# Reciprocal square roots as a power on POOL in a two-layer hybrid decoder trunk

## The chip, the cores and the metric

The kernel runs on one core of a Trainium2 chip. The metric is the device time of one execution in microseconds (us); of the kernel before the median of three runs is 1027.44. Engines are named as in the profile: PE or TensorE (matmul), PEld (its weight load), DVE or VectorE, ACT or ScalarE, POOL or GpSimd, SP or SyncE (it issues the weights' transfers). `L401` is line 401 of the kernel before; the changed kernel has line numbers of its own.

## The reference

A trunk of two decoder layers over 256 tokens of 1024 features, all in float32. A layer, cut to what matters:

```
xn = rms_norm(h) ;  u = xn @ W_in
o_A = RG-LRU branch ; o_B = Conformer branch (a norm inside)
o_C = differential attention, 4 heads:
      q, k = rope(rms_norm(q)), rope(rms_norm(k))        # per head of 64
      o = rms_norm((softmax1 - lambda * softmax2) @ v)   # per head of 128
o_D = sparse attention, 4 heads: rms_norm of q, k and the indexer's key
h += W_o(sum_j sigmoid(xn @ W_g[j]) * (o_j @ W_b[j]))
h += W_down(silu(g) * v),  [g, v] = dwconv3(rms_norm(h) @ W_up)
h += sigmoid(rms_norm(h) @ W_pg) * rms_norm(p @ W_p)

def rms_norm(x, gain):
    y = x * lax.rsqrt(mean(x * x) + 1e-6)
    return y * gain
```

## The kernel before, in words

**The main stream.** All weights, 340 pieces of mostly 128 x 1024 numbers, pass once through TensorE. SP fetches a piece to `raw` (5 buffers), ACT rounds it to `hi` (`L244`), VectorE subtracts to `lo` (`L245`); `hi` and `lo` have 6 buffers each, and pieces are prepared 3 ahead of their use (`LEAD`). A product is the sum of three: hi by hi, hi by lo, lo by hi (`mm3`, `L317` to `L319`, with the 256 tokens as columns, and `tok_unit`, `L360` to `L362`, with 512 features as columns). Its result lies in one of four PSUM banks (`mm`); four more banks (`sp`) serve all the rest.

**The side work.** The branches are generators: `side_a` (RG-LRU), `side_b` and `conv` (Conformer), `side_c` (differential attention), `side_d` (sparse attention). Between the pieces of the main stream `pump` advances them, each by its own interval (`EVERY`). So their small instructions lie between the main stream's, on the same engines. A scheduler then fixes one queue for each engine, in order; an instruction that waits holds up all that stands behind it in its queue.

**Where the roots are.** `root` (`L400`) makes 1/sqrt(scale * sums + bias) from an ACT root (`L401`) and a VectorE reciprocal (`L402`). It is called ten times on 128 x 2: in `Norm.finish`, in `rnorm` and for the norm of the PLE gate. In `rnorm` and after a norm TensorE first sums the squares over partitions (`L408`), then `root`, then TensorE spreads the two columns over all partitions (`spread`, `L395`). `side_d` has a root over 128 x 12 (`L690`, `L691`), `side_c` one over 128 x 32, for two blocks of 128 tokens, q and k, 8 heads each (`L838`, `L839`), and one over 128 x 8 for the attention's results (`L922`, `L923`). ACT loads a table (ACT_TABLE_LOAD) when the function that it needs next is not in the one that it has.

**`side_c` around the roots.** The squares are made on ACT (`L835`) and summed on VectorE (`L836`), block by block. Behind the root, `L841` makes `qs`, the factors of the queries, from it; ACT applies the factors of the keys head by head (`L850`). The attention's scores (`L881`) need both; `L885` and `L886` take the maximum, `L890` makes the exponentials, `L893` to `L897` the difference of the two softmaxes. `L903` transposes it, and `L911` multiplies by the values. `L916` squares the results, which the root `L922` turns to factors, and `L929` applies these.

**Beside it.** `side_d` makes its indexer's scores on TensorE (`L737`) into four `sp` banks, ACT takes them out (`L741`), VectorE weighs and sums them (`L745`, `L747`) and finds the largest (`L754`, `L755`). `L1010` is a step of the Conformer's convolution on VectorE; `L1092` adds a branch's product on ACT.

Of the kernel before, what the change touches and what calls it, by code (L numbers as in the profile page):

```python
# [10 lines left out]
F32 = mybir.dt.float32  # L11
F32R = mybir.dt.float32r
BF16 = mybir.dt.bfloat16
AF = mybir.ActivationFunctionType
ALU = mybir.AluOpType
# [3 lines left out]
P = 128  # L19
# [110 lines left out]
def decoder_kernel(ctx: ExitStack, tc: tile.TileContext, w_dram, x_dram, xt_dram, p_dram, vec_dram, row_dram,  # L130
                   gain_dram, lru_dram, const_dram, out_dram):
    nc = tc.nc
    A, V, T = nc.scalar, nc.vector, nc.tensor

    cst = ctx.enter_context(tc.tile_pool(name="cst", bufs=1))
# [16 lines left out]
    def bt(tag="big", bufs=NBIG, dtype=F32):  # L152
        return big.tile([P, 2, S], dtype, name=nm("b"), tag=tag, bufs=bufs)

    def st(shape, tag, bufs=1, dtype=F32):
        return sm.tile(shape, dtype, name=nm("s"), tag=tag, bufs=bufs)
# [18 lines left out]
    h = [[cst.tile([P, 512], F32, name=f"h{b}{n}", tag=f"h{b}{n}") for n in range(2)] for b in range(2)]  # L175
# [7 lines left out]
    eps = cst.tile([P, 3], F32, name="eps", tag="eps")  # L183
    V.memset(eps[:, 0:1], EPS)
    V.memset(eps[:, 1:2], 4 * EPS)

    def cc(name):
        o, w = _C[name]
        return con[:, o:o + w]
# [208 lines left out]
        return rs  # L398

    def root(rt, sums, scale, bias):  # L400
        A.activation(rt, sums, AF.Sqrt, scale=scale, bias=bias)  # L401
        V.reciprocal(rt, rt)  # L402

    def rnorm(acc, scale, bias):

        t = smbank()
        for b in range(2):
            T.matmul(t[:, 0, b:b + 1], acc[:, 0, b * P:(b + 1) * P], ones[:, 0:1], start=True, stop=True)  # L408
        rt = st([P, 2], "rt", 4)
        root(rt, t[:, 0, 0:2], scale, bias)  # L410
        return rt, spread(rt)

    class Norm:
# [40 lines left out]
        def finish(self):  # L454
            self.rt = st([P, 2], "rt", 4)
            V.tensor_tensor(self.ss[:, 0, :], self.ss[:, 0, :], self.ss[:, 1, :], op=ALU.add)
            root(self.rt, self.ss[:, 0, :], 1.0 / D, eps[:, 0:1])
# [115 lines left out]
    for l in range(L):  # L573
# [79 lines left out]
        def weave(gens):  # L653

            live = list(gens)
            while live:
                for g in list(live):
                    if next(g, "end") == "end":
                        live.remove(g)
                    else:  # L660
                        yield
# [15 lines left out]
        def side_d():  # L677
            dq, dk, ik = raws["dq"], raws["dk"], raws["ik"]
            ms = st([P, 2, 6], "msd", 1)
            for b in range(2):  # L680
# [6 lines left out]
                j = st([P, P], "junk", 2)  # L687
                A.activation(j[:, 0:32], ik[b][:, 0:32], AF.Square, scale=32 ** -0.5, accum_out=ms[:, b, 5:6])
                yield
            A.activation(ms, ms, AF.Sqrt, bias=eps[:, 0:1])  # L690
            V.reciprocal(ms, ms)  # L691
            qs = st([P, 2, 4], "qsd", 1)
            V.tensor_scalar(qs, ms[:, :, 0:4], P ** -0.5, None, op0=ALU.mult)
            yield
# [134 lines left out]
        def side_c():  # L829
            cq, ck, cv = raws["cq"], raws["ck"], raws["cv"]  # L830
            ms = st([P, 2, 2, 8], "msc", 1)
            for b in range(2):
                for i, t in enumerate((cq, ck)):
# [1 line left out]
                    A.activation(j, t[b], AF.Square, scale=0.125)  # L835
                    V.tensor_reduce(ms[:, b, i, :], j.rearrange("p (h w) -> p h w", h=8), axis=AX.X, op=ALU.add)  # L836
                    yield
            A.activation(ms, ms, AF.Sqrt, bias=eps[:, 0:1])  # L838
            V.reciprocal(ms, ms)  # L839
            qs = st([P, 2, 8], "qs", 1)  # L840
            V.tensor_scalar(qs, ms[:, :, 0, :], 0.125, None, op0=ALU.mult)  # L841
            yield
# [23 lines left out]
            mo = st([P, 2, 4], "mo", 1)  # L866
# [52 lines left out]

            yield from weave([*two_heads(1), attend(0, (0, 1))])  # L920
            yield from weave(attend(1, (hp,)) for hp in range(2))
            A.activation(mo, mo, AF.Sqrt, bias=eps[:, 0:1])  # L922
            V.reciprocal(mo, mo)  # L923
            oc = [(bt(dtype=F32R), bt(dtype=F32R)) for _ in range(2)]
            o_pairs[2] = oc
            for b in range(2):
# [4 lines left out]
            for b in range(2):  # L931
# [4 lines left out]
                for i in range(2):  # L936
# [3 lines left out]
                                           op1=ALU.subtract)  # L940
# [120 lines left out]
        t = st([80, S], "ikc", 1)  # L1061
# [96 lines left out]
        for g2 in range(NG // 2):  # L1158
            cf = st([P, 4, S], "e4", 2)
            pair = bt()  # L1160
            for q in range(2):
# [7 lines left out]
                for s_ in range(2):  # L1169
                    c = g + s_ * NG  # L1170
                    A.activation(cf[:, 2 * q + s_, :], bank[:, s_, :], AF.Identity, scale=w[:, 3 * c + 2:3 * c + 3],  # L1171
                                 bias=bb[:, c:c + 1])
                for d in (1, 2):
                    for s_ in range(2):
                        c = g + s_ * NG
                        t = cf[:, 2 * q + s_, d:]
                        V.scalar_tensor_tensor(t, bank[:, s_, :S - d], w[:, 3 * c + 2 - d:3 * c + 3 - d], t,  # L1177
                                               op0=ALU.mult, op1=ALU.add)
# [28 lines left out]
        for n in range(2):  # L1207
# [5 lines left out]
            for b, c, bank in parts:  # L1213
                cs = slice(c, c + bank.shape[1])
                t = bt().rearrange("p a b -> p (a b)")[:, cs]
# [104 lines left out]
```

## Time and profile before

| | |
|---|---|
| median of 3 runs | 1027.44 us (1027.05 to 1027.67) |
| the profiled execution | 1026.79 us, its span 1025.0 us |
| granted TensorE clock | 1.00 |
| PE busy | 1017.8 us |
| DVE busy | 832.1 us |
| ACT busy | 687.3 us |
| POOL busy | 0.2 us |
| HBM | 182.46 MB read, 179 GB/s over the span |

The span is what the profile sees of the execution, the rest of its time lies ahead of the first instruction and behind the last. Busy times are sums over the whole span; what a stage waits for is read from that stage. The profile's page has five parts that matter here: busy times, the chain that ended last, the costliest groups, the waits, and the timeline of a window, where a row in brackets tells how long the engine stood idle ahead of it and what ended that.

### The profile page before, as it was taken

Reading aid. Unit: us, or ns where it says so; the run is one execution under the profiler, and the core shown is the slowest. Engines: PE = TensorE matmul, PEld = TensorE weight load, DVE = VectorE, ACT = ScalarE, POOL = GpSimd, SP = SyncE. Lnnn points to the kernel's source line nnn. Section 1 sums busy time; section 2 is a strip of 40 time slices with the busy share of each in tenths; the row PEclk is TensorE's granted clock in tenths of the full one; section 3 lists DMA queues with packets and bytes.
Section 4 is the critical chain, followed back from the end, with each engine's and each line's share of the span. In section 5 each row is a group of like instructions: output and inputs, shape, how many; then the busy total and the mean of one; then the engine's idle time right before and its main releaser. Section 6 shows DMA issues by size and latency. Waiting matters only on the chain.

```text
span 1025.0 us, 16548 instructions
## 1 busy us (share of the span) xinstructions
PE 1017.8 (99%) x6108; PEld 896.5 (87%) x6108; DVE 832.1 (81%) x1530; ACT 687.3 (67%) x1190; POOL 0.2 (0%) x4
## 2 busy tenths in 40 slices
PE   9999999999999999999999999999999999999998
PEld 9988787888889999988899887888788899999887
DVE  7898999968869988765676989999687899887454
ACT  8688685977467766554765786859764776665443
POOL 0000000000000000000000000000000000000000
PEclk9999999999999999999999999999999999999999
DMA  8665844653538566476653657445446466566651
GB/s 288 236 192 167 278 140 146 184 161 121 199 108 305 160 206 188 145 256 188 189 178 119 207 167 224 144 147 183 144 153 196 144 207 184 186 186 185 188 162 42
DMA packets 53936, 184.58 MB, mean 180 GB/s; under 512 B 6112, under 2 KB 8160, under 8 KB 53856
## 3 DMA queue, kind: packets, MB, share of 16 engines
q1 hardware_dynamic: 53712, 183.52, 57.1%
q8 instruction: 48, 0.79, 0.3%
q14 instruction: 32, 0.26, 0.1%
q10 hardware_dynamic: 144, 0.00, 0.0%
HBM read 182.46 MB, written 1.05 MB: 179 GB/s over the span
## 4 chain that ended last, share of the span: by engine, by line
PE 92%; DVE 4%; ACT 2%; issue 1%; DMA 1%; SPq 0%; ACTq 0%
PE mm L360 17%; PE mm L361 17%; PE mm L362 17%; PE mm L319 11%; PE mm L317 11%; PE mm L318 11%; DVE lo L245 1%; PE mm L383 1%; DVE b L1010 1%; PE sp L451 1%; PE sp L797 1%; PE sp L911 1%; PE sp L881 1%; DVE s L755 1%; PE sp L821 1%
## 5 line engine op out<-in xcount | busy, mean ns | idle before, releaser
L244 ACT ACTIVATE hi<-raw 128x1024 fp32r<-128x1024 f32 (+1 forms) x340 | 352.8, 1048 | 210.4 <-PE mm L362 128.0
L245 DVE TENSOR_TENSOR lo<-raw,hi 128x1024 fp32r<-128x1024 f32 (+1 forms) x340 | 407.4, 1206 | 98.9 <-ACT hi L244 96.8
L360 PE MATMUL mm<-hi,b 128*128 128x512 f32 x848 | 337.2, 398 | 0.1
L361 PE MATMUL mm<-lo,b 128*128 128x512 f32 x848 | 330.8, 390 | 0.0
L362 PE MATMUL mm<-hi,b 128*128 128x512 f32 x848 | 330.3, 390 | 0.0
L319 PE MATMUL mm<-b,lo 128*128 128x256 f32 x960 | 271.4, 283 | 0.5 <-DVE lo L245 0.4
L317 PE MATMUL mm<-b,hi 128*128 128x256 f32 x960 | 271.4, 284 | 0.3 <-DVE b L440 0.2
L318 PE MATMUL mm<-b,hi 128*128 128x256 f32 x960 | 271.0, 283 | 0.0
L360 PEld LDWEIGHTS mm<-hi,b 128*128 128x128 f32 x848 | 159.4, 188 | 35.3 <-issue 1.1
L362 PEld LDWEIGHTS mm<-hi,b 128*128 128x128 f32 x848 | 159.2, 188 | 33.7
L361 PEld LDWEIGHTS mm<-lo,b 128*128 128x128 f32 x848 | 159.5, 188 | 31.5 <-issue 0.5
L319 PEld LDWEIGHTS mm<-b,lo 128*128 128x128 f32 x960 | 184.1, 192 | 1.2 <-DVE lo L245 1.1
L317 PEld LDWEIGHTS mm<-b,hi 128*128 128x128 f32 x960 | 183.7, 192 | 1.2 <-DVE b L440 0.6
L318 PEld LDWEIGHTS mm<-b,hi 128*128 128x128 f32 x960 | 184.1, 192 | 0.3 <-DVE b L441 0.2
L1010 DVE SCALAR_TENSOR_TENSOR b<-s,vec,b 128x256 f32<-128x256 f32 x240 | 104.8, 475 | 0.0
L1177 DVE SCALAR_TENSOR_TENSOR s<-mm,vec,s 128x255 f32<-128x255 f32 (+1 forms) x144 | 59.7, 474 | 5.7 <-ACT s L1171 5.7
L303 ACT ACTIVATE b<-b 128x512 fp32r<-128x512 f32 x40 | 25.0, 626 | 21.4 <-DVE b L1181 19.0
L1171 ACT ACTIVATE s<-mm,vec 128x256 f32<-128x256 f32 x72 | 36.1, 551 | 2.5 <-PE mm L319 2.5
L304 DVE TENSOR_TENSOR b<-b,b 128x512 fp32r<-128x512 f32 x40 | 27.4, 687 | 12.6 <-ACT b L303 12.6
L890 ACT ACTIVATE s<-sp,s,s 128x128 f32<-128x128 f32 (+1 forms) x32 | 15.9, 512 | 15.2 <-DVE s L886 14.9
L491 DVE TENSOR_TENSOR b<-mm,s 128x512 f32<-128x512 f32 x24 | 16.3, 683 | 11.1 <-PE mm L319 11.0
L1180 ACT ACTIVATE s<-s 128x256 f32<-128x256 f32 x44 | 17.8, 409 | 10.0 <-DVE s L1177 10.0
(229 smaller groups left out, 783.2 us busy)
## 6 DMA issues: line engine op xcount, KB each, us to landing
raw<-in_w_dram SPq DMA_DIRECT2D x332, 512.0 KB, 4.2
raw<-in_w_dram SPq DMA_DIRECT2D x8, 256.0 KB, 5.0
b<-in_x_dram SPq DMA_DIRECT2D x8, 128.0 KB, 4.5
b<-in_lru_dram SPq DMA_DIRECT2D x4, 256.0 KB, 4.9
h<-in_xt_dram SPq DMA_DIRECT2D x4, 256.0 KB, 6.2
gain<-in_gain_dram SPq DMA_DIRECT2D x2, 512.0 KB, 5.8
out_dram<-h SPq DMA_DIRECT2D x3, 256.0 KB, 2.3
row<-in_row_dram SPq DMA_DIRECT2D x2, 272.0 KB, 5.5
```

The costliest lines, as they stand in the source:

```text
L244: A.activation(hi[:, cs], raw[:, cs], AF.Copy)
L245: last_lo[0] = V.tensor_tensor(lo[:, cs], raw[:, cs], hi[:, cs].bitcast(F32), op=ALU.subtract).ins
L304: V.tensor_tensor(lo, src, hi.bitcast(F32), op=ALU.subtract)
L317: T.matmul(out, a, xh, start=first and k == 0, stop=False)
L318: T.matmul(out, a, xl, start=False, stop=False)
L319: T.matmul(out, b, xh, start=False, stop=last and k == nk - 1)
L360: T.matmul(outs[b], xk[k][0][:, bs], wh[:, kk, :], start=k == 0, stop=False)
L361: T.matmul(outs[b], xk[k][0][:, bs], wl[:, kk, :], start=False, stop=False)
L362: T.matmul(outs[b], xk[k][1][:, bs], wh[:, kk, :], start=False, stop=last)
L1010: V.scalar_tensor_tensor(t, ypad[:, c, d:d + S], w[:, 31 * c + d:31 * c + d + 1], t, op0=ALU.mult, op1=ALU.add)
L1171: A.activation(cf[:, 2 * q + s_, :], bank[:, s_, :], AF.Identity, scale=w[:, 3 * c + 2:3 * c + 3], bias=bb[:, c:c + 1])
L1177: V.scalar_tensor_tensor(t, bank[:, s_, :S - d], w[:, 3 * c + 2 - d:3 * c + 3 - d], t, op0=ALU.mult, op1=ALU.add)
```

## The change

A tile `half_power` of 16 columns of -0.5 is made once. `root` is now a VectorE `tensor_scalar` (times scale, plus bias) and, on POOL, a `tensor_tensor` with `pow` of it and `half_power`, in place. The three roots of the attentions go through a new function `roots`, which calls `root` for each block of 128 tokens, so 128 x 12 becomes two of 128 x 6, 128 x 32 two of 128 x 16, 128 x 8 two of 128 x 4. That makes 22 powers in all: 10 of 2 columns, 4 each of 6, 16 and 4. The square root of the RG-LRU (`L986`) stays on ACT. On ACT 16 table loads are left of 36.

```diff
--- before.py
+++ after.py
@@ -184,6 +184,9 @@
     V.memset(eps[:, 0:1], EPS)
     V.memset(eps[:, 1:2], 4 * EPS)
 
+    half_power = cst.tile([P, 16], F32, name="half_power", tag="half_power")
+    V.memset(half_power, -0.5)
+
     def cc(name):
         o, w = _C[name]
         return con[:, o:o + w]
@@ -398,8 +401,13 @@
         return rs
 
     def root(rt, sums, scale, bias):
-        A.activation(rt, sums, AF.Sqrt, scale=scale, bias=bias)
-        V.reciprocal(rt, rt)
+        V.tensor_scalar(rt, sums, scale, bias, op0=ALU.mult, op1=ALU.add)
+        nc.gpsimd.tensor_tensor(rt, rt, half_power[:, 0:rt.shape[1]], op=ALU.pow)
+
+    def roots(t):
+
+        for b in range(2):
+            root(t[:, b, :], t[:, b, :], 1.0, eps[:, 0:1])
 
     def rnorm(acc, scale, bias):
 
@@ -687,8 +695,7 @@
                 j = st([P, P], "junk", 2)
                 A.activation(j[:, 0:32], ik[b][:, 0:32], AF.Square, scale=32 ** -0.5, accum_out=ms[:, b, 5:6])
                 yield
-            A.activation(ms, ms, AF.Sqrt, bias=eps[:, 0:1])
-            V.reciprocal(ms, ms)
+            roots(ms)
             qs = st([P, 2, 4], "qsd", 1)
             V.tensor_scalar(qs, ms[:, :, 0:4], P ** -0.5, None, op0=ALU.mult)
             yield
@@ -835,8 +842,7 @@
                     A.activation(j, t[b], AF.Square, scale=0.125)
                     V.tensor_reduce(ms[:, b, i, :], j.rearrange("p (h w) -> p h w", h=8), axis=AX.X, op=ALU.add)
                     yield
-            A.activation(ms, ms, AF.Sqrt, bias=eps[:, 0:1])
-            V.reciprocal(ms, ms)
+            roots(ms.rearrange("p b i h -> p b (i h)"))
             qs = st([P, 2, 8], "qs", 1)
             V.tensor_scalar(qs, ms[:, :, 0, :], 0.125, None, op0=ALU.mult)
             yield
@@ -919,8 +925,7 @@
 
             yield from weave([*two_heads(1), attend(0, (0, 1))])
             yield from weave(attend(1, (hp,)) for hp in range(2))
-            A.activation(mo, mo, AF.Sqrt, bias=eps[:, 0:1])
-            V.reciprocal(mo, mo)
+            roots(mo)
             oc = [(bt(dtype=F32R), bt(dtype=F32R)) for _ in range(2)]
             o_pairs[2] = oc
             for b in range(2):
```

Since the factors of a block no longer wait for those of the other, and since ACT has fewer instructions, the scheduler writes the queues in another order. Three places follow. Names left of the arrow are written, those right of it read.

**ACT's queue at the root of `side_c`, layer 0, before** (`s_1451` are the factors, `L741` takes the scores of `side_d` out of PSUM):

```order
L244 ACTIVATE hi_1573<-raw_1572 128x1024
L741 ACTIVATE s_1487<-sp_1475 128x256
L741 ACTIVATE s_1487<-sp_1476 128x256
L741 ACTIVATE s_1487<-sp_1477 128x256
L741 ACTIVATE s_1487<-sp_1478 128x256
L1092 ACTIVATE b_1548<-mm_1399,s_507 128x512
L1092 ACTIVATE b_1550<-mm_1400,s_507 128x512
L835 ACTIVATE b_1598<-b_1293 128x512
L244 ACTIVATE hi_1602<-raw_1601 128x1024
L838 ACT_TABLE_LOAD
L838 ACTIVATE s_1451<-s_1451,eps 128x32
L741 ACTIVATE s_1535<-sp_1523 128x512
```

and now (`L748` is what `L741` was, `L856` what `L850` was, `L842` what `L835` was, `L1097` what `L1092` was; `s_1455` are the factors):

```order
L247 ACTIVATE hi_1577<-raw_1576 128x1024
L856 ACTIVATE b_1295<-b_1295,s_1455 128x64
L748 ACTIVATE s_1491<-sp_1479 128x256
L748 ACTIVATE s_1491<-sp_1480 128x256
L748 ACTIVATE s_1491<-sp_1481 128x256
L748 ACTIVATE s_1491<-sp_1482 128x256
L856 ACTIVATE b_1295<-b_1295,s_1455 128x64 x7
L1097 ACTIVATE b_1552<-mm_1403,s_509 128x512
L1097 ACTIVATE b_1554<-mm_1404,s_509 128x512
L842 ACTIVATE b_1602<-b_1297 128x512
L247 ACTIVATE hi_1606<-raw_1605 128x1024
L748 ACTIVATE s_1539<-sp_1527 128x512
```

Eight `L856`, which read the factors of the first block of tokens, now stand among the work of `side_d`, one of them ahead of the first four `L748`, and seven ahead of `L1097` and `L842`. The table load is gone.

**VectorE's queue at the same place, before** (`L841` reads the factors, `L839` is the reciprocal):

```order
L245 TENSOR_TENSOR lo_1603<-raw_1601,hi_1602 128x1024
L750 TENSOR_TENSOR s_1473<-s_1473,con 128x128
L550 TENSOR_TENSOR s_4935<-s_4935 128x4
L754 MAX s_1650<-s_1473 128x8
L839 RECIPROCAL s_1451<-s_1451 128x32
L755 MATCH_REPLACE s_1474<-s_1650,s_1473 128x128
L841 TENSOR_SCALAR s_1625<-s_1451 128x16
L745 TENSOR_SCALAR s_1521<-s_1535,s_1207 128x256
```

and now (`L404` is the new `tensor_scalar`, of the second block; `L847` is what `L841` was, `L754` what `L747` was):

```order
L248 TENSOR_TENSOR lo_1607<-raw_1605,hi_1606 128x1024
L752 TENSOR_SCALAR s_1525<-s_1539,s_1211 128x256
L404 TENSOR_SCALAR s_1455<-s_1455,eps 128x16
L754 SCALAR_TENSOR_TENSOR s_1525<-s_1539,s_1211,s_1525 128x256
L847 TENSOR_SCALAR s_1631<-s_1455 128x16
L757 TENSOR_TENSOR s_1477<-s_1477,con 128x128
L754 SCALAR_TENSOR_TENSOR s_1525<-s_1540,s_1211,s_1525 128x256
```

Between the root's own instruction and the reader of the factors stood one `MATCH_REPLACE`, now one `L754`; the power itself is in POOL's queue, between the two.

**ACT's queue at the second block of queries of the differential attention, layer 0, before** (`L890` are the exponentials):

```order
L916 ACTIVATE s_2187,s_1855<-b_1853 128x128
L1092 ACTIVATE b_2235<-mm_2083,s_507 128x512
L1092 ACTIVATE b_2237<-mm_2084,s_507 128x512
L778 ACTIVATE b_1204<-sp_2207,vec_75 128x2x128
L778 ACTIVATE b_1205<-sp_2207,vec_75 128x2x128
L781 ACTIVATE s_1206<-sp_2214 128x128
L244 ACTIVATE hi_2327<-raw_2326 128x1024
L890 ACTIVATE s_2218,s_2217<-sp_2219,s_2217,s_1625 128x256 x2
L890 ACTIVATE s_2218,s_2217<-sp_2220,s_2217,s_1625 128x256 x2
```

and now (`L922` is what `L916` was, `L934` what `L929` was, `L896` what `L890` was, `L785` and `L788` what `L778` and `L781` were; `s_1861` are the factors of the results):

```order
L922 ACTIVATE s_2193,s_1861<-b_1859 128x128
L1097 ACTIVATE b_2241<-mm_2089,s_509 128x512
L934 ACTIVATE b_1859<-b_1859,s_1861 128x128
L1097 ACTIVATE b_2243<-mm_2090,s_509 128x512
L785 ACTIVATE b_1208<-sp_2213,vec_75 128x2x128
L785 ACTIVATE b_1209<-sp_2213,vec_75 128x2x128
L788 ACTIVATE s_1210<-sp_2220 128x128
L247 ACTIVATE hi_2333<-raw_2332 128x1024
L934 ACTIVATE b_1859<-b_1859,s_1861 128x128 x3
L896 ACTIVATE s_2224,s_2223<-sp_2225,s_2223,s_1631 128x256 x2
L896 ACTIVATE s_2224,s_2223<-sp_2226,s_2223,s_1631 128x256 x2
```

The four `L934` of the first block of tokens, which read its power, moved from behind the attention into this place, the first of them between the two `L1097`. On VectorE the `tensor_scalar` ahead of that power stands behind the `lo` of a piece and ahead of the maxima `L891` (before `L885`) of this block.

On TensorE, `spread` at the start of layer 1 (`L395`) stands 13 matmuls earlier than before, and in `rnorm` of both layers the sum `L408` stands four matmuls earlier, with 3 matmuls of the main stream between it and `L395`, where 7 were. POOL's queue had four memsets; now it has the 22 powers behind them, and ahead of the first power one instruction (ISA) that names the library of the code it needs.

## Rows read from the trace of the kernel before

**Rows 1.** The page, part 1: busy time, share of the span and instructions of each engine.

```profile
PE 1017.8 (99%) x6108; PEld 896.5 (87%) x6108; DVE 832.1 (81%) x1530; ACT 687.3 (67%) x1190; POOL 0.2 (0%) x4
```

**Rows 2.** The waits of TensorE: us in total, times, the longest.

```profile
PE mm L319 <- DVE lo L245: 0.4, 2, 0.2
PE sp L903 <- DVE s L897: 0.4, 1, 0.4
PE sp L395 <- DVE s L402: 0.3, 1, 0.3
```

**Rows 3.** Lines 401, 402, 839: duration ns min/median/max, first and last start.

```profile
L401 ACT ACT_TABLE_LOAD  x6: 1283/1283/1283, 17.6 to 1000.0; - x6
...
L402 DVE RECIPROCAL s<-s x10: 155/166/166, 19.5 to 1001.7; 128x2 f32<-128x2 f32 x10
...
L839 DVE RECIPROCAL s<-s x2: 334/338/343, 132.0 to 646.2; 128x32 f32<-128x32 f32 x2
```

**Rows 4.** Groups of instructions on POOL: busy us, mean ns of one.

```profile
L1308 POOL MEMSET const-float32-0.0<- 128x1 f32 x1 | 0.1, 98 | 0.2 <-issue 0.2
```

**Rows 5.** Busy time by window, layer 0 from `side_c` to the first `L903`.

```profile
123.00:178.00 55.00, 55.00 (x285) 44.38 (x283) 54.54 (x176) 38.52 (x79) 0.00 (x0) 1.00 0.47 149
```

**Rows 6.** Timeline of layer 0 around `side_c`: start us, duration us, [idle before <-releaser].

```profile
124.50 1.19 ACT L741 ACTIVATE s<-sp 128x256 f32<-128x256 f32 x4
126.45 1.37 ACT L1092 ACTIVATE b<-mm,s 128x512 f32<-128x512 f32 x2 [0.77 <-PE mm L362]
127.72 0.62 ACT L835 ACTIVATE b<-b 128x512 f32<-128x512 f32 x1
...
132.74 0.83 ACT L850 ACTIVATE b<-b,s 128x64 f32<-128x64 f32 x3
...
122.08 1.21 DVE L245 TENSOR_TENSOR lo<-raw,hi 128x1024 fp32r<-128x1024 f32 x1
...
125.77 0.28 DVE L745 TENSOR_SCALAR s<-s,s 128x128 f32<-128x128 f32 x1
...
129.44 0.68 DVE L836 TENSOR_REDUCE s<-b 128x8 f32<-128x512 f32 x1
...
133.03 0.47 DVE L747 SCALAR_TENSOR_TENSOR s<-s,s,s 128x256 f32<-128x256 f32 x1
...
127.03 1.15 PE L737 MATMUL sp<-s,s 32*128 32x256 f32 x16
```

**Rows 7.** The same around the second block of queries of the differential attention.

```profile
188.88 1.24 ACT L1092 ACTIVATE b<-mm,s 128x512 f32<-128x512 f32 x2
...
190.89 1.07 ACT L244 ACTIVATE hi<-raw 128x1024 fp32r<-128x1024 f32 x1
192.70 0.57 ACT L890 ACTIVATE s<-sp,s,s 128x256 f32<-128x256 f32 x1 [0.73 <-DVE s L886]
...
193.26 0.55 ACT L890 ACTIVATE s<-sp,s,s 128x256 f32<-128x256 f32 x1
...
230.88 0.68 ACT L929 ACTIVATE b<-b,s 128x128 f32<-128x128 f32 x2
...
189.84 1.21 DVE L245 TENSOR_TENSOR lo<-raw,hi 128x1024 fp32r<-128x1024 f32 x1
...
195.26 1.14 PE L881 MATMUL sp<-b,b 64*128 64x256 f32 x8
```

**Rows 8.** The same in layer 1, VectorE.

```profile
635.30 1.23 DVE L245 TENSOR_TENSOR lo<-raw,hi 128x1024 fp32r<-128x1024 f32 x1 [0.95 <-ACT hi L244]
...
686.40 1.22 DVE L245 TENSOR_TENSOR lo<-raw,hi 128x1024 fp32r<-128x1024 f32 x1 [0.60 <-ACT hi L244]
```

**Rows 9.** The same at the first norm, TensorE.

```profile
18.36 0.50 PE L408 MATMUL sp<-ones,b 128*128 128x1 f32 x4
...
21.53 0.60 PE L395 MATMUL sp<-con,s 128*128 128x128 f32 x4
```

**Rows 10.** The page, part 6: DMA issues, KB each, median us to landing.

```profile
raw<-in_w_dram SPq DMA_DIRECT2D x332, 512.0 KB, 4.2
```

## Prediction, made before the changed kernel was run

> **What bounds the kernel now.** I read the busy times first. TensorE is busy for 1017.8 of the span's 1025.0 us and VectorE for 832.1; POOL, the engine that gets the new work, for 0.2 [rows 1]. So at most 7.2 us can be won anywhere, and then only where TensorE stands still. The view of its waits came next: 0.4 us behind `lo` of `L245`, 0.4 behind `L897`, and 0.3 behind the reciprocal of a norm, at the start of layer 1 [rows 2]. Only that last one is a wait for a root. Of the operations that go, the reader should see that none is expensive for TensorE: the table loads take 1.283 us each, all on ACT, and the reciprocals 0.16 to 0.34 us on VectorE [rows 3].
>
> Then I asked which engine has no slack behind TensorE. From 123 to 178 us VectorE is busy for 54.54 of 55.00 us [rows 5], and at the end of this stretch TensorE waits for it at `L903` [rows 2]. A microsecond that VectorE loses in there is a microsecond that TensorE loses. Layer 1 repeats the stretch with two idle times of VectorE in it, 0.95 and 0.60 us, both behind `hi` of `L244` [rows 8].
>
> **The unknown price.** No row shows a power on any engine. POOL's nearest row is a memset of one column, 98 ns [rows 4]. For a short elementwise operation whose time hardly grows with its columns the nearest rows are VectorE's reciprocals: 0.166 us for 2 columns, 0.338 for 32, under 6 ns a column [rows 3]. The low end is therefore 0.1 us whatever the width. As the high end I take two memsets for a column and two for the start, 0.2 + 0.2n. Below 0.1 us nothing is to be had, since the shortest row of POOL takes that. A power is no single multiply or add, so I expect a cost for each column, and take **one memset for the start and one for each column, 0.1 + 0.1n us**: 0.3 for the norms' 2 columns, 0.5 for the differential attention's 4, 0.7 for the sparse attention's 6, 1.7 for `side_c`'s 16.
>
> What a two-input elementwise instruction costs on this engine is in the Trainium skill (GPSIMD Engine Reference, 3.1 Elementwise): about 2.6 cycles an element, and VectorE roughly twice as quick. No run here shows it. Applied to the power it gives an estimate of 35 ns for 16 columns over the start, so the sum would be that of the cheap rival below; the same section tells writers to leave elementwise work to VectorE.
>
> **Layer 0, `side_c` (16 columns).** Terms (a) to (d) are delays of VectorE between 123 and 178 us.
>
> (a) The first power can start when VectorE is done with `L245` (122.08 + 1.21 = 123.29) and with the new `tensor_scalar` (0.16, as the reciprocal): 123.45. It ends at 125.15. ACT's queue now has an `L850` that needs it ahead of the four `L741`, which began at 124.50 [rows 6]. With its 0.28 (0.83 for three) they begin at 125.43: 0.9 late. The first ends about 125.85; `L745`, which needs it, began at 125.77. Cost 0.1. The last ends at 125.43 + 1.19 = 126.6, before TensorE wants its bank for `L737` at 127.03 [rows 6], so TensorE itself is spared.
>
> (b) Then seven more `L850` (7 x 0.28 = 1.9) stand ahead of the two `L1092` (1.37) and `L835` (0.62): 126.6 + 1.9 + 1.4 + 0.6 = 130.5. VectorE came to `L836`, which needs `L835`, at 129.44 [rows 6]; with (a), (d) and the multiplications of a rotation that now stand ahead it comes at about 129.9. Cost 0.6.
>
> (c) The second power is issued behind `L836`. `L841` needs it, and only one `L747` (0.47) now lies between the `tensor_scalar` and `L841`. VectorE stands still for 1.7 - 0.45 = 1.25, with all its queue behind it.
>
> (d) Four more `tensor_scalar` and two reciprocals less: 4 x 0.16 - 0.2 - 0.33 = 0.1. Some of the next layer's small constants move ahead of `L897`, two of 0.16. Together 0.4, rounded down to 0.3, as issues overlap.
>
> Sum 0.1 + 0.6 + 1.25 + 0.3 = 2.25, which arrives whole at `L903`.
>
> **Layer 0, attention (4 columns).** The squares of the first block of queries used to wait for those of the second. Now VectorE makes their `tensor_scalar` behind `L245` (189.84 + 1.21 = 191.05), so the power ends at 191.05 + 0.16 + 0.5 = 191.7. ACT has an `L929` that needs it right behind the first `L1092` (188.88 + 0.57 = 189.45) and stands for 2.25 us. Behind it wait the second `L1092` and all up to the end of `L244`, 189.45 to 191.96, which is 2.5 us of work, and the four `L929`, 0.68 for two, in a row about 0.3 apart [rows 7]. The first `L890` so begins at 191.7 + 0.3 + 2.5 + 0.9 = 195.4 and not 192.70: 2.7 late. The second `L881` writes at 195.26 + 0.27 into a bank that the second `L890` gives free at 193.26 + 0.55 = 193.81 [rows 7]: 1.7 of slack. Cost 2.7 - 1.7 = 1.0.
>
> **Layer 1.** The same with three differences. `L1092` loses a table load ahead of `L835`, so I leave out (b). (a) is 0.2. VectorE's idle 0.60 us in front of `L245` takes as much of the delay back; the 0.95 lies ahead of the power's harm and takes nothing [rows 8]. So 0.2 + 1.25 + 0.3 - 0.6 + 1.0 = 2.15.
>
> **The norms (2 columns) and `side_d` (6).** `tensor_scalar` and power take 0.16 + 0.3; the pair before took a root on ACT and a reciprocal of 0.17, and in six of ten cases a table load of 1.28 as well [rows 3]. The first norm has from 18.86 to 21.53 for it [rows 9]. At the start of layer 1 `L395` moves 13 matmuls forward while the load ahead of it goes: I leave the wait at its 0.3 [rows 2]. In `rnorm` 3 matmuls instead of 7 lie between `L408` and `L395`: I put 0.2 each on that, an estimate from the 0.3 that the power takes itself. `L474`, which halves a norm's factors on VectorE, now stands for those 0.3 us with the next `lo` behind it, but outside the stretch that is full [rows 5] pieces are ready ahead of their use, and I put nothing on it. In `side_d` an `L992` lies between the power and VectorE's use of it, and I put 0.1 on both layers. Sum 0.5. The table loads that vanish (36 in ACT's queue before, 16 after: 20 x 1.283 = 25.7 us [rows 3]) count as nothing, since ACT is not what TensorE waits for; if they had cover to give, it is spent in (b).
>
> **Sum:** 2.25 + 1.0 + 2.15 + 0.5 = **5.9 us**. The profiled execution took 1026.79 (its span 1025.0 and 1.8 around it), so it would take 1032.7; it lies 0.65 below the median of 1027.44, on which the forecast is **1033.3**. Low end of the price (0.1): (a), (b), (c) are nothing, (d) stays in layer 0 and goes into idle time in layer 1, the attention costs 1.0 - 0.4 = 0.6 in each: 0.3 + 0.6 + 0.6 = 1.5, 1028.9. High end (3.4 for 16 columns, 1.0 for 4): (a) 1.7, (b) 0.6, (c) 2.95, (d) 0.3, attention 1.5, together 7.05; layer 1 1.7 + 2.95 + 0.3 - 0.6 + 1.5 = 5.85; norms 1.1: 14 us, 1041.4.
>
> **Rivals.** *A power as cheap as the low end*: +1.5, 1028.9. For it speaks the slow growth of VectorE's own rows [rows 3].
>
> *Not slower.* If the power of 4 columns is there before ACT comes to `L929`, that is if VectorE's queue runs 2 us earlier against ACT than in rows 7, the attention costs nothing; and if 16 columns take under 0.45, (c) neither. Then the freed ACT can take the 0.3 of `L395` and the 0.4 of `L319` [rows 2] away: -0.7, 1026.7, which is no change that can be measured. Against it: in both layers `L245` and the `tensor_scalar` stand ahead of that power.
>
> *A dear power*, or one that each time waits for a VectorE instruction of the length of `L245`, 1.21 [rows 6], about the high end: 1041.4.
>
> *The first power is late.* Its code may have to be fetched; POOL's queue has a load of it ahead of the first power. A fetch like the weights' takes 4.2 us from issue to landing [rows 10]; the cover at the first norm is 21.53 - 18.86 - 0.16 - 0.3 = 2.2 [rows 9]. If it begins only there, 2.0 come on top: 1035.3. The Trainium skill (GPSIMD Engine Reference, 2.1 Instruction dispatch) gives about 6 us for the first call of freshly loaded code; by that estimate it would be 1037.1. No row shows such a load.
>
> **How the numbers follow.** Forecast 0.52, cheap 0.20, not slower 0.08, dear 0.13, first power late 0.07. A measurement tells about 0.2%, 2.05 us, from no change, so "same" is up to 1029.5: three quarters of the cheap case and most of the not-slower case, 0.21. Faster, 0.04: all the waits of rows 2 together would not reach it, so it needs something that no row shows. Slower 0.75. The range goes from 1028.0, which leaves out "not slower" and a little of the cheap case, to 1042.0, just over the high end.
>
> **What would show it.** POOL's rows give the price: 16 columns near 1.7 us, 4 near 0.5. Right steps: `L841` waits for POOL about 1.2 us in each layer; the first `L903` waits about 2 us longer in layer 0; ACT's `L929` waits for POOL about 2 us; TensorE stands at the second `L881`. ACT's busy time falls by about 25 us and the time does not. Wrong: 16 columns under 0.5 us, or TensorE with no longer stalls at `L903` and `L881`.

## The result, and the profile after

The changed kernel takes 1044.94 us (median of 4 runs, 1044.66 to 1045.25) against 1027.24 before (4 runs): 1.0173 times as long, 95% interval 1.016 to 1.0185. That is 17.7 us slower. The forecast was slower, 1033.3 us, with a range to 1042: the sign was right, the size less than half of what came, and the time lies outside the range.

The page of the changed kernel, the lines that answer to [rows 1]: busy times, the granted clock of TensorE in 40 slices, and the chain that ended last.

```profile
PE 1026.2 (98%) x6108; PEld 903.5 (87%) x6108; DVE 834.4 (80%) x1537; ACT 660.1 (63%) x1154; POOL 30.0 (3%) x26
...
PEclk9999989999999999999999999999999999999999
...
PE 74%; DVE 15%; ACT 5%; issue 2%; POOL 2%; DMA 1%; SPq 0%; DVEq 0%; POOLq 0%; ACTq 0%
```

The span grew from 1025.0 to 1043.2 us, by 18.2. TensorE has the same 6108 instructions, yet is busy for 1026.2 us and not 1017.8: 8.4 us of the 18.2 lie in its busy time, mostly in matmuls that last longer. The other 9.8 are time in which it stands (1043.2 - 1026.2 = 17.0 against 1025.0 - 1017.8 = 7.2). The row PEclk shows why the matmuls are longer: slice 6 (from about 130 us) has an 8 where every slice had a 9; the falls in layer 1 are too short to show there and come out in the windows below. Over the whole span the mean granted clock is 0.993, and it was 1.00: 0.007 x 1043.2 = 7.3 us of full speed are missing. ACT's busy time fell from 687.3 to 660.1 us, and it bought nothing.

The waits of TensorE, to be read beside [rows 2] (us in total, times, the longest; `L744` is what `L737` was, `L909` what `L903` was, `L398` `L395`, `L887` `L881`):

```profile
PE sp L744 <- ACT s L748: 4.2, 2, 2.5
PE sp L909 <- DVE s L903: 4.0, 2, 2.4
PE sp L398 <- POOL s L405: 1.9, 3, 1.0
...
PE sp L887 <- ACT s L896: 0.9, 1, 0.9
```

Four places, 11.0 us. What POOL took for its powers, from the timeline of POOL (start, duration, [idle before]):

```profile
19.41 0.70 POOL L405 TENSOR_TENSOR s<-s,half_power 128x2 f32<-128x2 f32 x1 [18.96 <-DVE s L404]
...
91.01 3.00 POOL L405 TENSOR_TENSOR s<-s,half_power 128x6 f32<-128x6 f32 x2 [70.90 <-DVE s L404]
...
125.11 2.90 POOL L405 TENSOR_TENSOR s<-s,half_power 128x16 f32<-128x16 f32 x1 [31.10 <-DVE s L404]
...
197.76 1.01 POOL L405 TENSOR_TENSOR s<-s,half_power 128x4 f32<-128x4 f32 x1 [59.13 <-DVE s L404]
...
644.66 3.74 POOL L405 TENSOR_TENSOR s<-s,half_power 128x16 f32<-128x16 f32 x1 [30.96 <-DVE s L404]
```

0.70 us for 2 columns, 1.5 for 6, 1.01 for 4, 2.90 to 3.74 for 16. The forecast's sum had 0.3, 0.7, 0.5 and 1.7.

The timeline of the changed kernel at the places of the forecast (VectorE, ACT, then TensorE):

```profile
92.75 0.25 DVE L709 SCALAR_TENSOR_TENSOR s<-s,s,row 128x32 f32<-128x32 f32 x1 [1.08 <-POOL s L405]
...
124.81 0.23 DVE L404 TENSOR_SCALAR s<-s,eps 128x16 f32<-128x16 f32 x1
...
126.30 1.23 DVE L248 TENSOR_TENSOR lo<-raw,hi 128x1024 fp32r<-128x1024 f32 x1
...
128.70 0.29 DVE L752 TENSOR_SCALAR s<-s,s 128x128 f32<-128x128 f32 x1 [1.17 <-ACT s L748]
...
132.85 0.69 DVE L843 TENSOR_REDUCE s<-b 128x8 f32<-128x512 f32 x1 [0.30 <-ACT b L842]
...
138.67 0.17 DVE L847 TENSOR_SCALAR s<-s 128x16 f32<-128x16 f32 x1 [2.79 <-POOL s L405]
...
128.05 0.35 ACT L856 ACTIVATE b<-b,s 128x64 f32<-128x64 f32 x1 [3.60 <-POOL s L405]
...
198.80 0.40 ACT L934 ACTIVATE b<-b,s 128x128 f32<-128x128 f32 x1 [2.61 <-POOL s L405]
...
128.72 2.89 PE L744 MATMUL sp<-s,s 32*128 32x256 f32 x16 [1.77 <-ACT s L748]
...
134.27 0.63 PE L363 MATMUL mm<-hi,b 128*128 128x512 f32 x1
...
185.25 1.12 PE L909 MATMUL sp<-con,s 128*128 128x128 f32 x4 [1.50 <-DVE s L903]
...
204.85 0.48 PE L363 MATMUL mm<-hi,b 128*128 128x512 f32 x1
...
649.11 1.95 PE L744 MATMUL sp<-s,s 32*128 32x256 f32 x16 [2.46 <-ACT s L748]
...
705.15 1.17 PE L909 MATMUL sp<-con,s 128*128 128x128 f32 x4 [2.45 <-DVE s L903]
```

and the same instructions of TensorE before, where [rows 6, 7] do not have them:

```profile
178.61 0.33 PE L903 MATMUL sp<-con,s 128*128 128x128 f32 x1 [0.40 <-DVE s L897]
...
196.48 0.48 PE L360 MATMUL mm<-hi,b 128*128 128x512 f32 x1
...
637.71 1.15 PE L737 MATMUL sp<-s,s 32*128 32x256 f32 x16
...
688.74 0.33 PE L903 MATMUL sp<-con,s 128*128 128x128 f32 x1
```

The starts, set side by side, show how the delay of TensorE grows:

| instruction of TensorE | before | after | later by |
|---|---|---|---|
| second group of `L737` / `L744`, layer 0 | 127.03 | 128.72 | 1.7 |
| `L903` / `L909`, layer 0 | 178.61 | 185.25 | 6.6 |
| first main matmul behind the second block of queries | 196.48 | 204.85 | 8.4 |
| second group of `L737` / `L744`, layer 1 | 637.71 | 649.11 | 11.4 |
| `L903` / `L909`, layer 1 | 688.74 | 705.15 | 16.4 |
| end of the span | 1025.0 | 1043.2 | 18.2 |

A stand of TensorE does not end when the awaited instruction comes. Windows of the changed kernel behind the stands (busy time and instructions of each engine; the number behind the brackets of POOL is the granted clock):

```profile
131.00:137.00 6.00, 6.00 (x18) 4.33 (x16) 4.57 (x12) 4.71 (x9) 1.49 (x1) 0.58 0.16 23
187.00:195.00 8.00, 8.00 (x44) 6.79 (x43) 8.00 (x14) 7.10 (x16) 0.00 (x0) 1.00 0.69 205
651.00:656.00 5.00, 5.00 (x16) 3.98 (x16) 4.75 (x19) 4.97 (x11) 0.17 (x1) 0.66 0.00 0
705.00:711.00 6.00, 5.85 (x19) 4.45 (x20) 6.00 (x12) 5.43 (x9) 0.00 (x0) 0.72 0.70 190
```

Behind the two stands at `L744` and behind the one at `L909` in layer 1 the granted clock is 0.58 to 0.72 over 5 or 6 us, a mixture of its two levels, 1.2 and 2.4 GHz. In the timeline a matmul of 512 columns then lasts 0.63 us (row 134.27) and not 0.39, as most of them do elsewhere. Behind `L909` in layer 0, where TensorE stood for 1.50 us by its row, the clock stayed at 1.00.

### The profile page after: what moved, and what is told of

Its sections match the earlier page's. It is cut to its first block, busy times and chain, and to the rows that moved or that the text cites. A ratio compares the mean times of both kernels' runs of the same rounds, so it can differ in the third digit from the quotient of the medians.

```text
span 1043.2 us, 16556 instructions
## 1 busy us (share of the span) xinstructions
PE 1026.2 (98%) x6108; PEld 903.5 (87%) x6108; DVE 834.4 (80%) x1537; ACT 660.1 (63%) x1154; POOL 30.0 (3%) x26
## 4 chain that ended last, share of the span: by engine, by line
PE 74%; DVE 15%; ACT 5%; issue 2%; POOL 2%; DMA 1%; SPq 0%; DVEq 0%; POOLq 0%; ACTq 0%
PE mm L363 12%; PE mm L365 12%; PE mm L364 12%; PE mm L320 11%; PE mm L322 11%; PE mm L321 11%; DVE lo L248 6%; DVE b L1015 4%; POOL s L405 2%; DMA raw<-in_w_dram 1%; DVE s L762 1%; PE mm L386 1%; PE sp L459 1%; DVE s L761 1%; ACT hi L247 1%
## 5 line engine op out<-in xcount | busy, mean ns | idle before, releaser
L248 DVE TENSOR_TENSOR lo<-raw,hi 128x1024 fp32r<-128x1024 f32 (+1 forms) x340 | 409.6, 1211 | 104.4 <-ACT hi L247 102.3
L405 POOL TENSOR_TENSOR s<-s,half_power 128x2 f32<-128x2 f32 (+3 forms) x22 | 29.8, 1358 | 989.2 <-DVE s L404 989.2
L896 ACT ACTIVATE s<-sp,s,s 128x128 f32<-128x128 f32 (+1 forms) x32 | 15.9, 516 | 17.7 <-DVE s L892 17.5
L499 DVE TENSOR_TENSOR b<-mm,s 128x512 f32<-128x512 f32 x24 | 16.4, 687 | 10.4 <-PE mm L322 10.4
```

Of the source, the lines that this page charges most:

```text
L248: last_lo[0] = V.tensor_tensor(lo[:, cs], raw[:, cs], hi[:, cs].bitcast(F32), op=ALU.subtract).ins
L405: nc.gpsimd.tensor_tensor(rt, rt, half_power[:, 0:rt.shape[1]], op=ALU.pow)
```

## The experiments

The theory after the result was: the price of the 16 columns in `side_c`, in front of ACT and VectorE, makes the loss, and the clock adds to it. Rivals: the new order of the queues makes it, or the ten norms do.

**1. Powers in the norms alone** (`norms_pow`). In `roots`' three places:

```diff
-            roots(ms)
+            A.activation(ms, ms, AF.Sqrt, bias=eps[:, 0:1])
+            V.reciprocal(ms, ms)
```

> Only the ten roots of the norms are powers; the three roots of the attentions are root and reciprocal again. Theory (the price of 16 columns, by way of L744 and L847, makes the loss): three waits for POOL at the spread (0.6, 1.1 and 0.7 us in the changed kernel) against 0.5 before, so +1 to +1.5 us, about 1028.5, granted clock 1.00, no wait at L744. Rival (the norms on the path make the loss): +5 us or more. Rival (only the new order of the queues makes it): about +1.

1028.78 us, 1.0016 times the kernel before (1.0007 to 1.0025): +1.6. The wait at the spread, TensorE:

```profile
PE sp L398 <- POOL s L405: 2.1, 3, 1.0
```

The norms are not the loss. Their three uncovered powers cost a little more than the 1 to 1.5 us that were expected. In `rnorm` the power was longer than elsewhere, for a reason that experiment 6 shows:

```profile
234.77 1.60 POOL L405 TENSOR_TENSOR s<-s,half_power 128x2 f32<-128x2 f32 x1 [214.75 <-DVE s L404]
```

**2. The new order without any power** (`split_act`). `roots` stays, block by block, but `root` is ACT's root and VectorE's reciprocal again:

```diff
-        V.tensor_scalar(rt, sums, scale, bias, op0=ALU.mult, op1=ALU.add)
-        nc.gpsimd.tensor_tensor(rt, rt, half_power[:, 0:rt.shape[1]], op=ALU.pow)
+        A.activation(rt, sums, AF.Sqrt, scale=scale, bias=bias)
+        V.reciprocal(rt, rt)
```

> No power at all: every root is ACT's square root and VectorE's reciprocal, but the attentions' roots are still made block by block, so the factors of the first block stand ahead of the indexer's scores in ACT's queue as in the changed kernel, with more table loads (42 against 36). Theory (price): no wait over 0.5 us at L744, granted clock 1.00, about +1 us, 1028.3. Rival (the order of the queues): most of the 17.7 us is still there, +8 us or more, with long waits at L744 and L909.

1027.26 us, ratio 1.0 (0.9991 to 1.001), not even the 1 us that was expected. An `L856` that needs the factors stands ahead of the `L748` here too, and no wait at `L744` is left among TensorE's waits. So at the root of `side_c` the order alone costs nothing; it costs when what stands in front comes late. At the attention's results the order is another than in the changed kernel (no `L934` stands ahead of the `L896`), so it was not tried there.

**3. A power in `side_c` alone** (`sidec_pow`): the change of `roots` for `side_c` only, all else as before.

> Only the root of the differential attention's queries and keys is a power, 4 instructions of 16 columns; all other roots as before. Theory (price): waits at L744 of about 2 us in at least one layer and at the first L909 of 1.5 to 2.5 us, the granted clock under 1.00 behind the longer of them, +10 to +13 us, about 1039. Rival (norms): +3 us or less.

1041.25 us, 1.0138 (1.0121 to 1.0155): +14.1, a little over the 10 to 13 that were expected, and the bulk of the loss from 4 of the 22 powers. TensorE's waits (`L912` is what `L903` was, `L747` what `L737` was):

```profile
PE sp L912 <- DVE s L906: 8.6, 2, 4.7
...
PE sp L747 <- ACT s L751: 0.4, 2, 0.2
```

The wait at `L747`, expected to be 2 us in one layer, was 0.4 in both together; TensorE pays at `L912` instead. What VectorE waits for from 120 to 186 us:

```profile
DVE s L850 <- POOL s L412: 2.2, 1, 2.2
DVE s L755 <- ACT s L751: 1.3, 1, 1.3
```

Without the powers of `side_d` ahead of it, `side_c`'s first power starts at 123.70 us and not at 125.11, and ACT is late for VectorE (`L755`, 1.3) but not for TensorE. The same delay is paid further down.

**4. All powers but those of `side_c`** (`no_sidec`): one line of the change undone, as in experiment 1.

> All roots are powers but that of the differential attention's queries and keys, which is root and reciprocal again. Theory (price): no wait at L744, granted clock 1.00 all the way, +4 to +6 us, about 1032: the norms' 1 to 1.5, the block-by-block factors of the results about 1 in each layer at L887, the rest at L909. Rival (norms): over +10 us.

1032.12 us, 1.0049 (1.0034 to 1.0064): +4.9, as expected, and no wait at the place of `L744`. But the clock was not at 1.00 all the way, as had been expected: behind a stand of 1.69 us in layer 0 (at `L910`, which is `L903` of the kernel before) it is 0.72 over 6 us.

```profile
179.68 1.12 PE L910 MATMUL sp<-con,s 128*128 128x128 f32 x4 [1.69 <-DVE s L904]
...
180.00:186.00 6.00, 6.00 (x21) 4.66 (x21) 6.00 (x11) 5.35 (x9) 0.00 (x0) 0.72 0.66 210
```

The parts (1.6 of the norms, 3.3 more with `side_d` and the attention's results, 14.1 of `side_c`) add up to 19.0 against 17.7 measured together.

**5. A shorter power in `side_c`** (`sidec_narrow`), on top of experiment 3:

```diff
-            nc.gpsimd.tensor_tensor(u, u, half_power[:, 0:u.shape[1]], op=ALU.pow)
+            nc.gpsimd.tensor_tensor(u[:, 7:9], u[:, 7:9], half_power[:, 0:2], op=ALU.pow)
```

> As sidec_pow, but each of the four powers of side_c is made on 2 of the 16 columns only (columns 7 and 8, so that the first L850 and qs still wait for it); the other 14 columns of the factors stay without their power, so part of the computation is left out. Theory (the price by column): POOL takes 0.7 us and not 2.9 to 3.1, and +14 us becomes +1 to +4, 1028.5 to 1031, with the granted clock at 1.00 in layer 1. Rival (any wait for POOL in front of these queues costs the same, whatever its length): stays within 3 us of sidec_pow's 1041.

1031.54 us (1029.46 to 1031.64), 1.0036 (1.0024 to 1.0049): +4.5 and not +14.1, just over the range that was expected. The four powers take 0.7 to 0.9 us each. But their time is not all that changed. Most factors of the keys now have no power to wait for, and the first multiplication in ACT's queue (`L859`, which was `L850`) starts with VectorE's `L411`, while the power is still running:

```profile
123.71 0.73 POOL L412 TENSOR_TENSOR s<-s,half_power 128x2 f32<-128x2 f32 x1 [123.27 <-DVE s L411]
...
123.72 0.35 ACT L859 ACTIVATE b<-b,s 128x64 f32<-128x64 f32 x1 [1.81 <-DVE s L411]
```

where in experiment 3 it waited for POOL:

```profile
126.67 0.35 ACT L859 ACTIVATE b<-b,s 128x64 f32<-128x64 f32 x1 [2.03 <-POOL s L412]
```

VectorE's wait for the power, at `L850`, is left, and is 0.6 us in layer 0 instead of 2.2. So the run shows what the long powers cost by both queues together; that any wait for POOL costs the same, whatever its length, it speaks against for VectorE's queue only. (Experiment 1 does too: three waits for powers of 0.7 to 1.6 us cost 1.6 in all.) The clock was at 1.00 in layer 1, as expected; in layer 0 it was 0.72 from 180 to 186 us, behind a stand of 1.93 us. The six times lie in two groups, near 1029.6 and near 1031.6; why is not shown.

**6. The price by itself** (`price`). Ahead of the kernel before, three times:

```diff
+        for w in (1, 2, 4, 8, 16, 32, 64):
+            nc.gpsimd.tensor_tensor(pz[:, 0:w], px[:, 0:w], py[:, 0:w], op=ALU.pow)
+        for w in (2, 16, 64):
+            nc.gpsimd.tensor_tensor(pz[:, 0:w], px[:, 0:w], py[:, 0:w], op=ALU.mult)
```

> The kernel before with 21 powers of 1 to 64 columns and 9 multiplications of 2, 16 and 64 columns on POOL at its start, which nothing reads. Theory: 0.39 + 0.157 us for each column (0.55, 0.70, 1.0, 1.6, 2.9, 5.4, 10.4); a multiplication of 16 columns well under 0.5 us; the time stays at 1027.2, since POOL's work disturbs neither VectorE nor ACT. Rival (the price is POOL's for any two-input instruction, not the power's): the multiplications cost the same. Rival (POOL and VectorE hinder each other): VectorE's instructions in the first 60 us become longer than before, and the powers longer where L245 runs.

1026.79 us, 0.9998 (0.9987 to 1.0008). Of each shape the shortest of three on POOL (`L194` is the power, `L196` the multiplication):

```profile
14.28 10.55 POOL L194 TENSOR_TENSOR pz<-px,py 128x64 f32<-128x64 f32 x1
...
31.19 2.90 POOL L194 TENSOR_TENSOR pz<-px,py 128x16 f32<-128x16 f32 x1
...
25.49 0.32 POOL L196 TENSOR_TENSOR pz<-px,py 128x64 f32<-128x64 f32 x1
...
25.18 0.22 POOL L196 TENSOR_TENSOR pz<-px,py 128x16 f32<-128x16 f32 x1
```

From 16 to 64 columns the power grows by (10.55 - 2.90) / 48 = 0.159 us a column. A multiplication of 16 columns takes 0.22 us, one of 64 takes 0.32, which is 0.002 us a column. So the price is that of the power, not of POOL as such. For the multiplication the rule of the Trainium skill (GPSIMD Engine Reference, 3.1 Elementwise), about 2.6 cycles an element, agrees: at the 1.2 GHz that the section reckons with it gives an estimate of 0.0022 us. The power's growth is some 75 times as large; the section gives the figure for an addition and none for a power.

One expectation was half wrong: VectorE hinders POOL, though a running power does not hinder VectorE in any measurable way. POOL and VectorE at 53 us (a power of 2 columns takes 0.70 us when left alone):

```profile
53.22 1.40 POOL L194 TENSOR_TENSOR pz<-px,py 128x2 f32<-128x2 f32 x1
...
52.84 1.22 DVE L256 TENSOR_TENSOR lo<-raw,hi 128x1024 fp32r<-128x1024 f32 x1
```

The power that started under VectorE's subtraction took 1.40 us: the 0.84 to the end of `L256` at 54.06, and 0.56 more. So it was 0.70 longer than alone, 0.14 less than what was left of `L256`. The Trainium skill (SBUF — State Buffer, SBUF: two separate sides) says that GpSimd and a VectorE instruction with two SBUF inputs share a pair of ports, and that the one that comes second waits for the whole of the other. This row agrees. So does the power of 3.74 us at 644.66 in the changed kernel:

```profile
644.40 1.24 DVE L248 TENSOR_TENSOR lo<-raw,hi 128x1024 fp32r<-128x1024 f32 x1
```

Of this `L248` 0.98 us were left, and the power took 0.84 more than 2.90, again 0.14 less. The power of 1.60 us in experiment 1 also started under an `L248`, which ran from 234.61 to 235.83. Where VectorE comes second to a power, the rows differ from the page: the `L248` at 126.30 in the changed kernel started in the middle of a power (125.11 to 128.01) and lasted 1.23 us, as long as any other. Under a multiplication, from 79.60 to 80.01 in this run, one `L256` did take 0.13 longer (1.35 us at 79.75).

**7. and 8. Stands of a known length** (`doses_a`, run a second time as `doses_a2`, and `doses_b`). On top of experiment 1, at three norms:

```diff
+        for _ in range(DOSE.get(calls[0], 0)):
+            nc.gpsimd.tensor_tensor(rt, rt, ones[:, 0:rt.shape[1]], op=ALU.pow)
+        calls[0] += 1
```

> norms_pow with further powers (exponent 1, same 2 columns, 0.7 us each) chained behind three of its ten roots: one in rnorm of layer 0, one at the start of layer 1, three in rnorm of layer 1, so that TensorE stands at the spread for about 1.3, 1.8 and 2.8 us. Theory (a long stand makes the granted clock fall to 1.2 GHz for some us): behind the third the matmuls of 512 columns come 0.43 us apart and not 0.227 for several us, behind the first two not; 1028.8 + 3.5 + about 2 = 1034.3. Rival (a stand costs its own length): 1032.3, and the clock stays at 1.00.

> As doses_a with two, two and six further powers: stands of about 2.0, 2.5 and 4.9 us. Theory (clock): the granted clock falls behind the second and third, perhaps the first, by 1.5 to 2.5 us each: 1028.8 + 7.0 + 3 to 6.5 = 1039 to 1042. Rival (own length): 1035.8.

> doses_a once more, with more executions, since its two lay 2.9 us apart. Theory (behind one and the same stand of 3 us the granted clock falls in some executions and in others not): the times lie in groups near 1032.2 and 1035 and few between. Rival (the two were an accident of the measurement): all within 0.5 us.

`doses_a` took 1032.24 and 1035.12 us, the second time 1033.68 to 1035.64 in four executions; `doses_b` 1039.72 and 1040.91. The sum without the clock was 1032.3 and 1035.8. So `doses_b` bears out the clock: about 4.5 us over the sum. In its profiled execution the stands were 1.85, 2.24 and 5.80 us, only 0.5 more in all than had been planned, and TensorE was busy for 1022.9 us, where experiment 1 had 1018.4. The two profiles of `doses_a` show one and the same place, behind the longest stand, first with 1032.24 us:

```profile
753.00:760.00 7.00, 7.00 (x36) 5.78 (x35) 3.83 (x8) 6.33 (x10) 0.00 (x0) 1.00 0.20 68
```

and then with 1035.64 us:

```profile
753.00:760.00 7.00, 6.86 (x26) 5.88 (x27) 2.46 (x6) 4.54 (x7) 0.08 (x1) 0.62 0.21 74
```

In one execution the clock is 1.00, in the other 0.62; TensorE's instructions in the 7 us are 36 and 26. The times did not fall into two groups as the theory had it, but lie scattered over 3.4 us: the stand itself differed too, 2.98 us in the one and 3.72 in the other. In the first the second of the three added powers began at 750.24, 0.02 ahead of an `L248`, and took 0.69 us; in the second it began at 750.56, 0.02 behind one, and took 1.76. But the length did not decide about the clock. In the second execution it fell some 2 us into the stand, with TensorE idle; in the first TensorE had stood as long by then, and the clock stayed. The same window, first with 1032.24 us and then with 1035.64:

```profile
751.00:752.00 1.00, 0.00 (x0) 0.00 (x0) 0.51 (x1) 0.00 (x0) 0.99 (x1) 1.00 0.86 299
...
751.00:752.00 1.00, 0.00 (x0) 0.00 (x0) 0.77 (x1) 0.00 (x0) 1.00 (x1) 0.74 0.91 283
```

So one and the same stand lowers the clock in one execution and not in another. In the traces of this study, the start of the kernel left aside, the stands up to 1.59 us all left it at 1.00, and of the 16 from 1.69 us on all lowered it but this one of 2.98. A length from which it always falls is not shown. The Trainium skill (TensorE: Matmul & The Clock Gate, What's actually happening) gives the two levels and says that the number of slow matmuls at a kernel's start differs from run to run, because the phase of the monitor that sets the clock is not tied to the kernel. The rows show such a difference in the middle of a kernel.

**9. and 10. Taking VectorE, then the order, out of it** (`sidec_qspool`, `sidec_once`). On top of experiment 3, first

```diff
-            V.tensor_scalar(qs, ms[:, :, 0, :], 0.125, None, op0=ALU.mult)
+            nc.gpsimd.tensor_scalar(qs, ms[:, :, 0, :], 0.125, None, op0=ALU.mult)
```

and then one power over both blocks:

```diff
-            roots(ms.rearrange("p b i h -> p b (i h)"))
+            mf = ms.rearrange("p b i h -> p (b i h)")
+            V.tensor_scalar(mf, mf, 1.0, eps[:, 0:1], op0=ALU.mult, op1=ALU.add)
+            nc.gpsimd.tensor_tensor(mf, mf, half_power, op=ALU.pow)
```

> As sidec_pow, but the multiplication that makes qs from the factors is on POOL too, behind the powers, so VectorE no longer stands at L847 for them (2.8 us in each layer of the changed kernel). Theory (VectorE, which has no slack up to L909, carries the delay): the waits at L909 fall by 2 to 3 us in each layer and the time by 4 to 6, to 1035 to 1037, and by more where the clock then does not fall. Rival (the delay comes only by way of ACT, from L856 ahead of L748): within 2 us of sidec_pow's 1041.3.

> As sidec_qspool, but with one power over all 32 columns (5.4 us), as the root was one instruction before: the key factors of the first block no longer stand ahead of L748 and ahead of the L1092 and L835 in ACT's queue. Theory: ACT then stands at L850 for some 5 us, but behind the indexer's work; no wait at L737; the time between 1031 and 1037. Rival (only the sum of the powers' time counts): no better than sidec_qspool.

1038.43 and 1038.84 us, both 1.0112 (1.0097 to 1.0127): only 2.8 and 2.4 less than experiment 3, where 4 or more had been expected. The one power of 32 columns took 6.36 us in layer 0, started under an `L248`, and 5.58 in layer 1. VectorE's waits from 120 to 186 us, first with `qs` on POOL:

```profile
DVE lo L248 <- ACT hi L247: 1.5, 1, 1.5
```

and with one power as well (`L513` is a rotation that reads the keys, `L861` what `L850` was):

```profile
DVE s L513 <- ACT b L861: 4.1, 1, 4.1
```

The wait at `qs` (2.2 us) is gone, and VectorE waits 1.5 us for `hi` of a piece instead, which ACT makes late because it stands for the factors itself. With one power all of the waiting is in one place, 4.1 us. The power's time reaches VectorE by whichever queue is left, and a change of the reader moves it and hardly shortens it.

**11. Powers only where they are covered** (`covered`). Experiment 1 with root and reciprocal at the three norms where TensorE waited:

```diff
+        calls[0] += 1
+        if calls[0] in (2, 6, 7):
+            A.activation(rt, sums, AF.Sqrt, scale=scale, bias=bias)
+            V.reciprocal(rt, rt)
+            return
```

> norms_pow with root and reciprocal again for three of the ten norms, those at whose spread TensorE waited for POOL (rnorm of both layers and the start of layer 1); the other seven stay powers of 2 columns. ACT then has 26 table loads, ten fewer than before (12.8 us). Theory (0.7 us of POOL costs nothing where other work covers it, and ACT's table loads are not what TensorE waits for): 1026.8 to 1027.5, as before. Rival (table loads are worth time): 2 us faster or more. Rival (each power costs something wherever it stands): 0.5 to 1 us slower.

1026.27 us, 0.9991 (0.9982 to 1.0): 0.9 us faster than the kernel before by the medians, with an interval that just reaches no change. That is 0.5 below the range that was expected. Seven powers of 0.7 us cost nothing, and ten table loads less gain at most 0.9 us. The page, part 1:

```profile
PE 1017.8 (99%) x6108; PEld 897.8 (88%) x6108; DVE 832.9 (81%) x1531; ACT 674.4 (66%) x1173; POOL 5.0 (0%) x11
```

ACT is busy for 674.4 us and not 687.3, TensorE as before. This is the fastest kernel of the study, by less than a measurement can well tell.

## Why the prediction was wrong in size

**What was right.** The mechanism and its places: `L841` behind POOL, `L903`, the second `L881`, ACT's `L929`. For the attention's results of layer 0 ACT was to stand 2.25 us and TensorE to lose 1.0; ACT stood 2.61 (row 198.80) and TensorE 0.9 at `L887`. That the sizes agree is partly luck: the power took 1.01 us and not 0.5, and at that price the sum had 1.5. In layer 1, where 1.0 had been put as well, ACT stood 1.03 us and TensorE not at all. The 25.7 us of table loads were costed at nothing, and experiments 2 and 11 bear that out, to within 0.9 us. `first power late` fell: the first took 0.70 us as all others.

**The first step that failed is the price.** "One memset for the start and one for each column, 0.1 + 0.1n us" is 1.7 for 16 columns; POOL took 2.90 at the least, and by its rows for 2 and 16 columns (0.70 and 2.90) about 0.39 + 0.157n. A memset of one column, the only row of that engine, says nothing of a power. The high end, 0.2 + 0.2n, came close, and had been given as a rival with a chance of 0.13. Experiment 3 shows that the four powers of 16 columns by themselves cost 14.1 us; experiment 5, with 0.7 to 0.9 us in their place, leaves 4.5, though there ACT's first wait went as well.

**Term by term.** (c) was 1.7 - 0.45 = 1.25; VectorE stood 2.79 us at the reader of the factors (row 138.67). (a) said that "TensorE itself is spared" at `L737`: in layer 0 ACT came to its first `L856` at 128.05 and not at 125.15, and TensorE stood 1.77 us (row 128.72). Two things fell together there, the price and `side_d`, on which I had put 0.1 us: its power held VectorE for 1.08 us (row 92.75), so `side_c`'s `tensor_scalar` came at 124.81 and not at 123.3; with the price and without `side_d`'s powers (experiment 3) TensorE stood 0.25 us there at most. In layer 1 (a) was put at 0.2 and TensorE stood 2.46 us (row 649.11): the power there met an `L248` and took 3.74. (b) was put at 0.6 and was 0.3 (row 132.85); that VectorE, late itself, came later to it is argued and not tried. (d) also counts instructions of `side_d` that run ahead of 123 us (the reciprocal at 94.88), which changes it by 0.1. The norms were put at 0.4 and cost 1.6 (experiment 1).

**The second step that failed is one that was missing.** The sum counts each stand at its own length. At the high end, near the price that came, it gave 14 us; the stands alone came to 9.8, less than that. The other 8.4 us lie in TensorE's busy time, some 7 of them by the lower clock behind three of the stands. (Some of the rest is in the groups of `L744`: in layer 1 its 16 matmuls took 1.95 us before the clock fell, and 1.15 in the kernel before.) [rows 5] show a granted clock of 1.00 over the whole stretch before, and no term of the sum lets it fall; in the changed kernel it fell behind stands of 1.77, 2.46 and 2.45 us. So with the right price the sum would have come nearer, but partly by accident: too much for the stands, nothing for the clock.

## What to carry to other kernels

Before work goes to an idle engine, put its very operation in that engine's queue, with the widths that are wanted and a result that nothing reads, and read its time: the kernel's time does not change, and one run gives the price. A result that comes late is not made harmless by choosing who waits for it first, when every reader's queue leads to an engine without slack. On a TensorE that is 99% busy a stand of about 2 us can cost twice its length, because the matmuls behind it may run at half the clock: by the table, the 2.45 us at `L909` in layer 1 were followed by 1.8 more up to the end.

## What the runs showed of the hardware that had not been expected

A power on POOL costs about 0.16 us for each column of 128 lanes and 0.4 to begin, some 75 times a multiplication's growth by column. A two-input instruction of POOL that starts under a two-input instruction of VectorE waits for its end (1.40 us for 0.70), while VectorE's own subtraction, started under a power, lasted as long as before (1.23 us). And a stand of TensorE lowered the granted clock about 2 us in in one execution, and left it at 1.00 for all of its 2.98 us in another.
